# A two-layer diffusion block in split fp32: instruction order at the seams between stages, and weight buffers in pools of one and two slots

## The chip, the cores and the metric

The kernel runs on one core of a Trainium2 chip. The metric is the device time of one execution in microseconds; where several were measured, the median counts. The kernel before took 3605.2 us as the median of 3 runs (3592.66 to 3619.01).

## What is computed

A block of two layers over 256 latent tokens and 256 context tokens of width 2048, in fp32. Layer 0 mixes tokens with a bidirectional RWKV-7 scan, layer 1 with Hyena (long convolutions by Fourier transforms with filters from a small network). Around each mixer, and around the squared-ReLU MLP behind it, stand RMS norms and the modulation by `c` (adaLN).

```python
for i in range(DEPTH):                      # DEPTH = 2; context lives in layer 0 only
    mod = silu(c) @ ada_w[i] + ada_b[i]      # six rows of 2048
    h = rms_norm(x, norm_g[i, 0]) * (1 + mod[1]) + mod[0]
    y = rwkv_mixer(h, hc, ...) if i == 0 else hyena_stream(h, ...)
    x = x + mod[2] * rms_norm(y, norm_g[i, 1])
    h = rms_norm(x, norm_g[i, 2]) * (1 + mod[4]) + mod[3]
    x = x + mod[5] * rms_norm(square(relu(h @ mlp_up[i])) @ mlp_down[i], norm_g[i, 3])

# rwkv_mixer: token shift xx, lora branches, keys, scan over tokens, readout
k = (h + xx * mu[2]) @ w_k ; v = (h + xx * mu[3]) @ w_v ; r = (h + xx * mu[0]) @ w_r
S = S * w_t - (S @ kk_t) b_t^T + v_t k_t^T ; o_t = S @ r_t      # per head, both directions
y = ((group_norm(o) + bonus) * gate) @ w_o
```

## The kernel before, in words

The whole block is one program of the class `Kern`. A scheduler orders the instructions of each engine when the program is built: it takes them in the order in which the code was traced, moved by priorities (`tc.high_priority(n)`); on the chip each engine then runs its own list in order. Side work (adaLN products, filters, mixes) comes as Python generators that `tick` advances a little at a time between pieces of the main work; `self.rate` says how fast.

**Products.** Each fp32 matmul is three products of halves: an operand is cast by ACT to a high half (`wh`, `xh`, `yh`) and DVE subtracts it for the low half (`wl`, `xl`, `yl`) in `split_into`; `mm3` makes hi·hi, hi·lo and lo·hi into one PSUM tile. `load_split` takes a raw weight buffer (`w`, 128x2048), loads it on SP's queue, and splits it in tiles of 128x1024 (`wh`, `wl`). Raw buffers and split tiles come from lists of pools, `self.wraw` and `self.wsp`; `turn` rotates the list, so that the pools are taken in turn, and a pool of n slots gives its next slot out again when the tile n turns before has been used up. `open_weights(es, raw, sp)` adds one pool to each list. Before, the stages from w_o on use one pair of pools (raw 2 slots, split 3), and each MLP adds a pair of its own (`MLPW`, raw 1, split 3).

**Stages**, with their times in the profiled execution. 0 to 196 us: `start`, adaLN rows (`ada_first`), norms (`rstd`), the shifted tokens (`sx`, `shifted`), and for each of 16 chunks k the mixes (`xt`, `xh`, `xl`) for the decay, the iclr and the gate branch, whose products accumulate in six PSUM tiles; for `k < KEARLY` the mix for w_k is made in the same loop. To 431: the hidden layer of the branches, the w_k product (`rwkv_proj`, `gemm_ws`), beside it adaLN products by DVE (`acc`, `ada_run`) and more mixes. To 555: `rwkv_begin`, the first fills of r and v (w_r, w_v products, `fl`) and the second halves of the lora branches (`self.low`). To about 1403: the scan in eight groups of four heads (`rwkv_scan`), operands `VU`, `NT`, `KB`, `ard`; its list is pinned in traced order on PE, ACT, DVE and SP. The last group has the Hyena filters beside it (`filters`: three sine layers, then eight pairs of products with w4, split in `w4h`, `w4l`, and transforms stored as `ko`); then the last readout. To 1506: `rwkv_out`, y loaded (`yt`), split (`yh`, `yl`) and multiplied by w_o (`gemm_tok`). Then `resid` (sum of squares `ss`, root, reciprocal, two diagonal matrices `dg`, by which PE transposes and scales y, then the sum into x and the next norm), the first MLP (to 2294), `resid`, Hyena (to 2828), `resid`, the second MLP (to 3586), `resid`.

**Order around the change.** SP's queue carries most loads, the weights' and the scan's, in one list; what waits at its head holds back all behind it. ACT has the casts, the PSUM copies, `aw` (an adaLN chunk scaled for POOL to add) and the squares; DVE has the subtractions and the mixes.

Of the kernel before, what the change touches and what calls it, by code (L numbers as in the profile page):

```python
# [18 lines left out]
P = 128  # L19
# [50 lines left out]
class Kern:  # L70
# [105 lines left out]
    def gemm_ws(self, W, K, ms, x, ntok, evac, lead=False):  # L176

        nk = K // P
        if lead:
            ps = [[self.mm.tile([P, 512], F32, name="mm") for _ in range(2)] for _ in range(2)]  # L180
            for k0 in range(0, nk, 4):
                w = [self.load_split(W[k0 * P : (k0 + 4) * P, m0 * P : (m0 + 2) * P].rearrange("(k p) n -> p k n", p=P), 4, 256)
                     for m0 in ms[:2]]
                for k in range(4):
                    for j in range(2):
                        for i in range(2):
                            self.mm3(ps[j][i][:, :ntok], self.cut(w[j][k], slice(i * P, (i + 1) * P)), x(k0 + k),
                                     k0 + k == 0, k0 + k == nk - 1)
                self.tick(self.rate)
            for j in range(2):  # L190
                for i in range(2):
                    evac(ms[j] + i, ps[j][i][:, :ntok])
            ms = ms[2:]
        for m0 in ms:
            ps = [self.mm.tile([P, 512], F32, name="mm") for _ in range(2)]
            for k0 in range(0, nk, 8):
                src = W[k0 * P : (k0 + 8) * P, m0 * P : (m0 + 2) * P].rearrange("(k p) n -> p k n", p=P)
                w = self.load_split(src, 8, 256)
                for k in range(8):
                    for i in range(2):  # L200
# [3 lines left out]
                self.tick(self.rate)  # L204
            for i in range(2):
                evac(m0 + i, ps[i][:, :ntok])

    def gemm_tok(self, W, x, evac, lead=False, stages=None):

        for ns in ((0, 1), (2,), (3,)) if lead else ((0,), (1,), (2,), (3,)):  # L210
            ps = {(n, tt): self.mm.tile([P, 512], F32, name="mm") for n in ns for tt in range(2)}
            for k0 in range(0, KT, 4):
                if stages and len(ns) > 1:
                    stages(k0)
                for n in ns:
                    w = self.load_split(W[k0 * P : (k0 + 4) * P, n * 512 : (n + 1) * 512].rearrange("(k p) n -> p k n", p=P), 4, 512)
                    for k in range(k0, k0 + 4):
                        for tt in range(2):
                            self.mm3(ps[n, tt], self.cut(x(k), slice(tt * P, (tt + 1) * P)), w[k - k0], k == 0, k == KT - 1)
                    self.tick(self.rate)  # L220
            for n in ns:
                for tt in range(2):
                    evac(n, tt, ps[n, tt])
# [118 lines left out]
    def ada_scan(self, n, pool):  # L342
# [4 lines left out]
        nc.vector.memset(wide, 0.0)  # L347
        nc.vector.tensor_copy(wide[:, :, 0], self.sc2[:, 0, :])
        pick = pool.tile([P, 2], F32, name="pick", bufs=1)
        nc.vector.memset(pick, 0.0)  # L350
        for j in range(4):
            nc.vector.tensor_tensor(pick, pick, self.ident[:, 32 * j : 32 * j + 2], op=ALU.add)
# [42 lines left out]
    def rstd(self, x, pool, acc=None, make=None):  # L395
# [7 lines left out]
        for k in range(len(x)):  # L403
            if make:
                make(k)
            sq = pool.tile([P, L], F32, name="sq", bufs=3)
# [21 lines left out]
    def resid(self, x, y, ss, layer, gi, ch, pool, nxt=None):  # L428
# [12 lines left out]
        for n in range(1, 4):  # L441
            nc.vector.tensor_tensor(ss[:, 0, :], ss[:, 0, :], ss[:, n, :], op=ALU.add)
        nc.scalar.activation(ss[:, 1, :], ss[:, 0, :], AF.Sqrt, bias=self.eps[:, 0:1], scale=1.0 / D)
        nc.vector.reciprocal(ss[:, 1, :], ss[:, 1, :])
        dg = pool.tile([P, 2, P], F32, name="dg", bufs=1)
        for tt in range(2):
            nc.vector.tensor_scalar(dg[:, tt], self.ident, ss[:, 1, tt : tt + 1], None, op0=ALU.mult)
# [33 lines left out]
    def filters(self, es):  # L481
# [3 lines left out]
        p2 = self.pool(es, "f2", 2)  # L485
        fw = p1.tile([33, 64], F32, name="fw")
# [10 lines left out]
        for m, (lhs, n) in enumerate(((fw[:], 64), (w23[:], 64), (w3[:].rearrange("p a b -> p (a b)"), P))):  # L497
# [13 lines left out]
            if m == 2:  # L511
                self.tables()
            yield
# [9 lines left out]
        dft = []  # L523
        for i, nm in enumerate(("dftc", "dfts")):
            dft.append(self.dft_load(nm, p1, p2, "hf", 3))
        w4s = []

        def load(i):
            dc, o = divmod(i, 2)
            if dc < 4:  # L530
                w4 = p2.tile([P, 512], F32, name="w4")
                for b in range(2):
                    c0 = (b * 2 + o) * D + dc * 512
                    nc.sync.dma_start(w4[64 * b : 64 * b + 64, :], I["f_w4"][0, :, c0 : c0 + 512])
                w4s.append(w4)

        def skip(i):
            dc, o = divmod(i, 2)
            if dc < 4:
                self.sk = p2.tile([P, 512], F32, name="sk", bufs=1)[0:1, :]  # L540
                nc.sync.dma_start(self.sk, I["skip"][0, o : o + 1, dc * 512 : (dc + 1) * 512])

        def window(dc):
            if dc < 4:
                self.win = p2.tile([P, 2, 512], F32, name="win", bufs=1)
                nc.sync.dma_start(self.win, I["window"][:, dc * 512 : (dc + 1) * 512].rearrange("(a p) d -> p a d", p=P))

        window(0), load(0), skip(0)

        def first(dc, o, e, put):  # L550

            if not e:
                w4 = w4s.pop(0)
                self.w4 = split2(w4)
                load(2 * dc + o + 1)
            for tt in range(2):
# [4 lines left out]
                if o and e and tt:  # L561
                    window(dc + 1)
                if e == 0 and tt == 0:
# [6 lines left out]

        def split2(x):
            return self.split_into(p2.tile([P, 512], F32R, name="w4h")[:], x[:], p2.tile([P, 512], F32R, name="w4l")[:])
# [85 lines left out]
    def shifted(self, k):  # L658
# [3 lines left out]
        t = self.xt.tile([P, 512], F32, name="sx", bufs=2)  # L662
# [85 lines left out]
    def rwkv_proj(self, l2, ad1):  # L748
# [6 lines left out]
        self.bg, self.rate = [self.beside(mixed, self.NLOW + 24, ad, n)], (self.NLOW + 24 + n) / 15  # L755
# [17 lines left out]
        self.gemm_ws(I["w_k"][0], D, range(0, KT, 2), lambda k: xs[k], 512, evk)  # L773
# [179 lines left out]
    def rwkv_begin(self):  # L953
# [5 lines left out]
        for _ in self.beside(itertools.chain(self.fill_v(0), self.fill_r(1)), 48, self.low, n - n // 8 + .1):  # L959
            self.tick(self.BEG)  # L960
# [3 lines left out]
    def rwkv_scan(self, es, prep_pools, ngroups=KT // 2):  # L964
# [13 lines left out]
        self.bg, self.rate = [], 0.0  # L978
        for _ in self.scan_products(0, 0):
# [3 lines left out]
        for i in range(2):  # L983
            self.scan_values(0, i)
        self.pins = {}
        for g in range(ngroups):
# [88 lines left out]
    def scan_open(self, es, prep_pools):  # L1075

        self.loaded, self.unit, self.rx, self.due = [], 0, [], []
        self.ard, self.yf, self.kbp = [None] * 2, [None] * 2, [None] * 2
        self.scan_operands(self.pool(es, "so0"), 0)
        self.ge = self.pool(es, "sge", 2)  # L1080
# [316 lines left out]
    def scan_readout(self, g):  # L1397
# [53 lines left out]
    def rwkv_out(self, xp):  # L1451
        nc, tc = self.nc, self.tc
        with tc.tile_pool(reuse_waits="tile", name="oy", bufs=16) as oy, tc.tile_pool(reuse_waits="tile", name="op", bufs=1) as op:
            ys = []
            for k0, n in ((0, 4), (4, 4), (8, 4), (12, 2), (14, 2)):
                hi = [oy.tile([P, L], F32R, name="yh") for _ in range(n)]
                lo = [oy.tile([P, L], F32R, name="yl") for _ in range(n)]
                t = oy.tile([P, 4, L], F32, name="yt", bufs=2)
# [3 lines left out]
            ss = op.tile([P, 4, 2], F32, name="ss")  # L1462

# [7 lines left out]
            self.resid(x, o, ss, 0, 1, 2, op, (0, 2, 3))  # L1471
            return x
# [40 lines left out]
    PRT = 1  # L1513
# [4 lines left out]
    KEARLY = 16  # L1518
# [7 lines left out]
    SLACK = 0  # L1526
# [127 lines left out]
    def start(self, ap, xp):  # L1654
# [16 lines left out]
        self.pins, self.pinned = {}, ("pe",)  # L1671
# [5 lines left out]
        for q in range(4):  # L1677
# [4 lines left out]
            for k in range(4 * q, 4 * q + 4):  # L1682
# [5 lines left out]
                sx = self.shifted(k)  # L1688
                for n, m in enumerate((1, 4)):
# [8 lines left out]
        self.xs += [self.mix_split(2, k, True, self.xm) for k in range(self.KEARLY, KT)]  # L1698
# [27 lines left out]
    def run(self):  # L1726
        nc, tc = self.nc, self.tc
        with ExitStack() as es:
# [141 lines left out]
```

## Time and profile before

| what | us |
|---|---|
| median of 3 runs | 3605.2 |
| the profiled execution's own time | 3607.2 |
| its span (granted clock 0.968) | 3605.3 |
| TensorE (PE) busy | 3326.2 |
| VectorE (DVE) busy | 2457.0 |
| ScalarE (ACT) busy | 1739.7 |
| GpSimd (POOL) busy | 435.0 |

The profile is of one execution. Its page gives each engine's busy time; the table by stage gives the same for windows of the span; the waits name an engine's instruction, what it waited for, and the sum, the count and the longest wait in us; the timeline gives one row for an instruction or a run of equal ones, with its start, its length, and in brackets the idle time ahead of it and what ended it; the chain lists what ended last. PEld is TensorE's weight load, which runs beside the matmuls, L111 the line on which all split products are recorded, L53 that of the ACT, DVE and SP instructions.

### The profile page before, as it was taken

What the parts mean: (1) busy time and instruction counts of PE and PEld (TensorE: products, weight loads), DVE (VectorE), ACT (ScalarE), POOL (GpSimd) and SP (SyncE); (2) the same over time, 40 slices, a digit from 0 to 9 for tenths busy, and PEclk for the clock granted to TensorE, in tenths of its full rate; (3) what the DMA queues carried; (4) which work ended last, traced back from release to release, by engine and by line L of the source; (5) the groups of instructions that cost most, each with busy time, mean ns of one, the idle gap of its engine ahead of it and who ended that gap; (6) DMA issues with size and microseconds to landing.
All of it is one profiled execution on the core that took longest, in us unless ns stands there. A gap on an engine that the chain in (4) does not pass through costs nothing.

```text
span 3605.3 us, 74531 instructions
## 1 busy us (share of the span) xinstructions
PE 3326.2 (92%) x30598; PEld 2904.8 (81%) x30598; DVE 2457.0 (68%) x3867; ACT 1739.7 (48%) x3069; POOL 435.0 (12%) x496
## 2 busy tenths in 40 slices
PE   6799978989989788999999999999999899999999
PEld 3477777878888666898978889899887798989897
DVE  4788675767767655687777776587787675555554
ACT  4454454544544444443434435566664663434343
POOL 0011121111111000000000002034441540000000
PEclk8999998999999989999999999999999999999999
DMA  9678798988988635688888887566665775555553
GB/s 305 229 232 266 252 329 252 282 267 262 288 269 267 194 124 184 198 269 280 257 286 259 283 268 233 164 221 219 222 209 182 244 249 191 183 187 187 187 185 120
DMA packets 587807, 836.79 MB, mean 232 GB/s; under 512 B 39551, under 2 KB 373280, under 8 KB 587464
## 3 DMA queue, kind: packets, MB, share of 16 engines
q1 hardware_dynamic: 556360, 718.76, 62.1%
q0 software_dynamic: 31104, 113.26, 10.0%
q8 instruction: 239, 3.92, 0.5%
q14 instruction: 104, 0.85, 0.1%
HBM read 777.31 MB, written 54.59 MB: 231 GB/s over the span
## 4 chain that ended last, share of the span: by engine, by line
PE 49%; DMA 21%; DVE 14%; ACT 6%; issue 6%; POOL 2%; SPq 1%; ACTq 0%; DVEq 0%; POOLq 0%
PE mm L111 34%; DMA aw<-in_ada_w 10%; PE fl L111 5%; PE sg L111 5%; PE sc L111 4%; DVE wl L53 3%; DMA w<-in_mlp_down 2%; DVE acc L53 2%; DMA w<-in_mlp_up 2%; POOL acc L325 2%; ACT wh L53 2%; DVE tmp L53 1%; ACT aw L53 1%; DVE d L53 1%; DMA a<-a 1%
## 5 line engine op out<-in xcount | busy, mean ns | idle before, releaser
L53 DVE TENSOR_TENSOR wl<-w,wh 128x1024 fp32r<-128x1024 f32 (+1 forms) x716 | 918.6, 1288 | 548.7 <-ACT wh L53 546.8
L53 ACT CAST wh<-w 128x1024 fp32r<-128x1024 f32 (+1 forms) x716 | 738.1, 1043 | 744.4 <-PE mm L111 436.2
L111 PE MATMUL mm<-hxh,wh 128*128 128x258 f32 x2816 | 803.5, 287 | 13.2 <-DVE nt L53 11.9
L111 PE MATMUL mm<-hxh,wl 128*128 128x258 f32 x2816 | 801.5, 285 | 6.8 <-DVE wl L53 6.7
L111 PE MATMUL mm<-hxl,wh 128*128 128x258 f32 x2816 | 799.4, 284 | 0.0
L111 PEld LDWEIGHTS mm<-hxh,wh 128*128 128x128 f32 x2816 | 534.2, 190 | 17.0 <-DVE nt L53 13.8
L111 PEld LDWEIGHTS mm<-hxh,wl 128*128 128x128 f32 x2816 | 534.1, 190 | 10.7 <-DVE wl L53 9.3
L111 PEld LDWEIGHTS mm<-hxl,wh 128*128 128x128 f32 x2816 | 536.3, 190 | 1.8
L325 POOL TENSOR_TENSOR acc<-acc,aw 128x512 f32<-128x512 f32 x180 | 274.9, 1528 | 1360.2 <-ACT aw L53 1254.1
L111 PE MATMUL mm<-wh,uh 128*128 128x512 f32 x1024 | 405.4, 396 | 1.0 <-DVE nt L53 1.0
L111 PE MATMUL mm<-wl,uh 128*128 128x512 f32 x1024 | 400.5, 391 | 4.2 <-DVE wl L53 4.1
L111 PE MATMUL mm<-wh,ul 128*128 128x512 f32 x1024 | 402.3, 393 | 0.0
L53 DVE SCALAR_TENSOR_TENSOR acc<-aw,sc,acc 128x512 f32<-128x512 f32 x300 | 225.3, 751 | 89.6 <-DMA aw<-in_ada_w 87.0
L111 PEld LDWEIGHTS mm<-wl,uh 128*128 128x128 f32 x1024 | 192.3, 188 | 51.1 <-DVE wl L53 8.3
L111 PEld LDWEIGHTS mm<-wh,ul 128*128 128x128 f32 x1024 | 192.1, 188 | 45.6
L111 PEld LDWEIGHTS mm<-wh,uh 128*128 128x128 f32 x1024 | 192.3, 188 | 42.5 <-DVE nt L53 1.4
L111 PE MATMUL fl<-fh,fx 128*128 128x256 f32 x1024 | 213.1, 296 | 9.9 <-DMA fx<-xv 8.4
L53 ACT ACTIVATE aw<-aw,sc 128x512 f32<-128x512 f32 x180 | 125.8, 719 | 138.1 <-DMA aw<-in_ada_w 137.6
L111 PEld LDWEIGHTS fl<-fh,fx 128*128 128x128 f32 x1024 | 168.2, 193 | 27.9 <-issue 14.0
L111 PE MATMUL fl<-flo,fx 128*128 128x256 f32 x512 | 146.0, 285 | 0.4 <-issue 0.4
L111 PE MATMUL sg<-ard,KB 64*64 64x64 f32 (+1 forms) x3584 | 131.1, 247 | 13.5 <-ACT yf L53 4.8
L111 PE MATMUL mm<-xl,wh 128*128 128x512 f32 (+1 forms) x320 | 131.7, 412 | 12.1 <-DVE xl L53 12.0
(352 smaller groups left out, 5871.8 us busy)
## 6 DMA issues: line engine op xcount, KB each, us to landing
aw<-in_ada_w SPq DMA_DIRECT2D x288, 512.0 KB, 5.7
w<-in_mlp_down SPq DMA_DIRECT2D x128, 1024.0 KB, 5.1
w<-in_mlp_up SPq DMA_DIRECT2D x120, 1024.0 KB, 6.0
fx<-xv POOLq DMA_DIRECT2D x128, 512.0 KB, 6.2
aw<-in_ada_w SPq DMA_DIRECT2D x192, 256.0 KB, 3.0
w<-in_hy_in_w SPq DMA_DIRECT2D x44, 1024.0 KB, 6.2
fx<-xr POOLq DMA_DIRECT2D x64, 512.0 KB, 5.6
w<-in_w_k SPq DMA_DIRECT2D x16, 1024.0 KB, 5.7
```

The source lines that it names most:

```text
L53: return self.kern.pin(self.key, f(*a, **kw))
L111: return self.pin("pe", self.nc.tensor.matmul(out, lhsT=lhsT, rhs=rhs, **kw))
L325: nc.gpsimd.tensor_tensor(acc, acc, w[:, a], op=ALU.add)
```

## The change

The arithmetic and the number of instructions stay the same, but for one more small activation. What changes:

- *First stages.* `KEARLY` 16 to 12: the last four mixes for w_k come behind the loop, from the kept `sx` tiles (now 4). `self.mixed`, behind which the adaLN loads of the next stage are placed, is now the last of these. `rstd` has five `sq` buffers. The first block of w_k goes to PSUM tiles of the pool `sc` and advances no side work; side work runs at a rate of /13 in place of /15.
- *Begin and scan.* `LOWS` moves the lora branches ahead; the first two `scan_values` (the `VU` loads) are traced ahead of the first products, at priority 1000, as are the constants of the scan's adaLN; all remaining filter and adaLN work is taken ahead of the last readout, which uses `sc` tiles for both pairs.
- *Filters.* The loads of w4, window, skip and transforms are issued earlier, and w4 is split one step ahead.
- *Products.* In the last chunk of a product the output blocks are finished one after the other (`gemm_ws` with lead: by j; `gemm_tok`: by token half); `PRT` 1 to 400 for the last evacuations and for the chain up to `dg`.
- *Buffers.* The stages from w_o on have two pairs of pools: one of raw 1 and split 2 slots, opened ahead of `rwkv_out`, and one of raw 1 and split 1; `rwkv_out` opens its own second pair behind `yt`. The MLPs add (1, 3) as before. Since `turn` rotates the list, `open_weights` now takes its pool out by identity.

```diff
-                l.append(self.pool(es, n, b))
-                es.callback(l.pop)
+                p = self.pool(es, n, b)
+                l.append(p)
+                es.callback(lambda l=l, p=p: l.pop(next(i for i, q in enumerate(l) if q is p)))
...
+                order = [(j, k) for k in range(4) for j in range(2)]
+                for j, k in sorted(order) if k0 == nk - 4 else order:
...
-            ps = [self.mm.tile([P, 512], F32, name="mm") for _ in range(2)]
+            ps = first or [self.mm.tile([P, 512], F32, name="mm") for _ in range(2)]
...
+                    pairs = [(k, tt) for k in range(k0, k0 + 4) for tt in range(2)]
+                    for k, tt in sorted(pairs, key=lambda p: p[1]) if k0 == KT - 4 else pairs:
+                        self.mm3(ps[n, tt], self.cut(x(k), slice(tt * P, (tt + 1) * P)), w[k - k0], k == 0, k == KT - 1)
...
+            with self.tc.high_priority(self.PRT if 3 in ns else 0):
+                for n in ns:
+                    for tt in range(2):
+                        evac(n, tt, ps[n, tt])
...
+        with self.tc.high_priority(self.PRT):
+            for n in range(1, 4):
+                nc.vector.tensor_tensor(ss[:, 0, :], ss[:, 0, :], ss[:, n, :], op=ALU.add)
+            nc.scalar.activation(ss[:, 1, :], ss[:, 0, :], AF.Sqrt, bias=self.eps[:, 0:1], scale=1.0 / D)
+            nc.vector.reciprocal(ss[:, 1, :], ss[:, 1, :])
+            for tt in range(2):
+                nc.vector.tensor_scalar(dg[:, tt], self.ident, ss[:, 1, tt : tt + 1], None, op0=ALU.mult)
...
+        def weights(i):
+            halves.append(split2(w4s.pop(0)))
+            load(i)
...
+        window(0), load(0), load(1), skip(0)
...
-                w4 = w4s.pop(0)
-                self.w4 = split2(w4)
-                load(2 * dc + o + 1)
+                self.w4 = halves.pop(0)
...
+                if e and tt and w4s:
+                    weights(2 * dc + o + 3)
...
-        t = self.xt.tile([P, 512], F32, name="sx", bufs=2)
+        t = self.xt.tile([P, 512], F32, name="sx", bufs=4)
...
-        for _ in self.beside(itertools.chain(self.fill_v(0), self.fill_r(1)), 48, self.low, n - n // 8 + .1):
+        for _ in self.beside(itertools.chain(self.fill_v(0), self.fill_r(1)), 48, self.low, self.LOWS * (n - n // 8)):
...
+        with self.tc.high_priority(self.PRS):
+            for i in range(2):
+                self.scan_values(0, i)
         for _ in self.scan_products(0, 0):
             pass
         self.load_to(3 + self.AHEAD)
         self.feed_open(ngroups)
-        for i in range(2):
-            self.scan_values(0, i)
...
+        take(fill, 99), take(ada, 99)
         for _ in late:
             due, self.due = self.due, []
-            take(fill, 2)
             for f in due:
                 f()
-        take(fill, 99), take(ada, 99)
...
-            tile_ = lambda: (self.sc if last and pi else self.sg).tile([P, 512], F32, name="sc" if last and pi else "sg")
+            tile_ = lambda: (self.sc if last else self.sg).tile([P, 512], F32, name="sc" if last else "sg")
...
     def rwkv_out(self, xp):
...
+            es = ExitStack()
+            self.open_weights(es, 1, 1)
...
+                t = oy.tile([P, 4, L], F32, name="yt", bufs=2)
                 hi = [oy.tile([P, L], F32R, name="yh") for _ in range(n)]
                 lo = [oy.tile([P, L], F32R, name="yl") for _ in range(n)]
-                t = oy.tile([P, 4, L], F32, name="yt", bufs=2)
...
+            nc.scalar.activation(op.tile([P, 2], F32, name="st"), t[:, 1, :2], AF.Sqrt, scale=0.0, bias=self.eps[:, 0:1])
...
+            es.close()
...
-    PRT = 1
+    PRT = 400
...
-    KEARLY = 16
+    KEARLY = 12
...
+    LOWS = 1.25
+    PRS = 1000
...
-        self.xs += [self.mix_split(2, k, True, self.xm) for k in range(self.KEARLY, KT)]
+        self.xs += [self.mix_split(2, k, True, self.xm, sxs[k]) for k in range(self.KEARLY, KT)]
...
-                self.open_weights(e1)
-                self.np = self.pool(e1, "np", 1, "right")
-                self.hx = [self.np.tile([P, KT, L + 2], F32R, name=n, bufs=1) for n in ("hxh", "hxl")]
+
+                self.np = self.pool(e1, "np")
+                self.open_weights(e1, 1, 2)
+                self.hx = [self.pool(e1, n, 1, "right").tile([P, KT, L + 2], F32R, name=n, bufs=1) for n in ("hxh", "hxl")]
                 xp = self.pool(e1, "xp", side="right")
                 if self.upto >= 2:
                     x = self.rwkv_out(xp)
+                self.open_weights(e1, 1, 1)
```

How the order of instructions moves, at three places. DVE at the end of the lora stage: `acc` is the adaLN accumulation, `xt` a mix from `sx` and `hall`, `xl` the low half of its split; the last 256-wide `xl` is the gate branch's last split. Before:

```order
L53 SCALAR_TENSOR_TENSOR acc<-aw,sc_92,acc 128x512
L53 TENSOR_TENSOR xl<-xt,xh 128x512
L53 SCALAR_TENSOR_TENSOR xt<-sx,cols,hall 128x256
L53 SCALAR_TENSOR_TENSOR acc<-aw,sc_92,acc 128x512
L53 TENSOR_TENSOR xl<-xt,xh 128x512
L53 SCALAR_TENSOR_TENSOR xt<-sx,cols,hall 128x512
L53 TENSOR_TENSOR xl<-xt,xh 128x256
```

And now:

```order
L53 SCALAR_TENSOR_TENSOR xt<-sx,cols,hall 128x256
L53 TENSOR_TENSOR xl<-xt,xh 128x512
L53 SCALAR_TENSOR_TENSOR xt<-sx,cols,hall 128x512
L53 TENSOR_TENSOR xl<-xt,xh 128x512
L53 TENSOR_TENSOR xl<-xt,xh 128x256
L53 SCALAR_TENSOR_TENSOR xt<-sx,cols,hall 128x512
```

No `acc` stands between the last splits any more, and the last mixes for w_k (the last row is one of them) follow the gate's split.

SP at the start of the scan: `VU` are the first groups' values, `r` the store of a fill, `fr` the fill's weights, `gate` a store of the lora branch. What leaves is marked -, what comes +:

```order
-L53 DMA fr<-in_w_v 128x2x256
-L53 DMA gate<-l2t 128x256
-L53 DMA fr<-in_w_v 128x2x256
+L53 DMA VU<-v 64x128 x12
 L53 DMA r<-fe 128x2x256
-L53 DMA fr<-in_w_v 128x2x256
-L53 DMA VU<-v 64x128 x12
+L53 DMA fr<-in_w_v 128x2x256 x3
 L53 DMA aw<-in_ada_w 128x4x256 x2
```

The twelve `VU` loads stand ahead of the store of `r` and of three `fr` loads.

ACT at the start of the last group: `wh<-w` are casts of w_o's weights, `yf`, `rhs`, `KR`, `VU` copies of the scan. Before:

```order
L53 COPY rows<-mm 128x256
L53 CAST wh<-w 128x1024 x3
L53 COPY yf<-sg 32x16x32 x2
L53 COPY rhs<-sc 128x256
L53 COPY KR<-sg 128x4x64 x2
L53 ACTIVATE VU<-sc 64x2x2x64 x2
L53 ACT_TABLE_LOAD
```

And now:

```order
L53 COPY rows<-mm 128x256
L53 COPY yf<-sg 32x16x32 x2
L53 COPY rhs<-sc 128x256
L53 COPY KR<-sg 128x4x64 x2
L53 ACTIVATE VU<-sc 64x2x2x64 x2
L53 ACT_TABLE_LOAD
L53 ACTIVATE fz_16942<-fa 64x256
L53 CAST dftch<-hf 128x512
L53 COPY Z<-sc 128x256
```

The three casts are gone from here; the casts of the transform (`dftch`) and of w4 stand earlier.

More of the change, by code (lines that the diff above doesn't have):

```diff
@@ L174, in split_into, with gemm_ws @@
         return hi, lo
-    def gemm_ws(self, W, K, ms, x, ntok, evac, lead=False):
+    def gemm_ws(self, W, K, ms, x, ntok, evac, lead=False, first=None):
         nk = K // P
@@ L203, in gemm_ws @@
                                  k0 + k == 0, k0 + k == nk - 1)
-                self.tick(self.rate)
+                if not first:
+                    self.tick(self.rate)
             for i in range(2):
                 evac(m0 + i, ps[i][:, :ntok])
+            first = None
     def gemm_tok(self, W, x, evac, lead=False, stages=None):
@@ L346, in ada_scan @@
         wide = pool.tile([P, KT, 32], F32, name="wide", bufs=1)
[L347 to L348 removed]
         pick = pool.tile([P, 2], F32, name="pick", bufs=1)
[L350 to L352 removed]
+        with self.tc.high_priority(self.PRS):
+            nc.vector.memset(wide, 0.0)
+            nc.vector.tensor_copy(wide[:, :, 0], self.sc2[:, 0, :])
+            nc.vector.memset(pick, 0.0)
+            for j in range(4):
+                nc.vector.tensor_tensor(pick, pick, self.ident[:, 32 * j : 32 * j + 2], op=ALU.add)
         todo = [(layer, ch, i, half, k4) for layer, ch, i in itertools.islice(self.ada_todo, n) for half in range(2) for k4 in range(4)]
@@ L405, in rstd @@
                 make(k)
-            sq = pool.tile([P, L], F32, name="sq", bufs=3)
+            sq = pool.tile([P, L], F32, name="sq", bufs=5)
             nc.scalar.activation(sq[:, :n], x[k], AF.Square)
@@ L485, in filters, with load, skip, window @@
         p2 = self.pool(es, "f2", 2)
+        w4s = []
+        def load(i):
+            dc, o = divmod(i, 2)
+            if dc < 4:
+                w4 = p2.tile([P, 512], F32, name="w4")
+                for b in range(2):
+                    c0 = (b * 2 + o) * D + dc * 512
+                    nc.sync.dma_start(w4[64 * b : 64 * b + 64, :], I["f_w4"][0, :, c0 : c0 + 512])
+                w4s.append(w4)
+        def skip(i):
+            dc, o = divmod(i, 2)
+            if dc < 4:
+                self.sk = p2.tile([P, 512], F32, name="sk", bufs=1)[0:1, :]
+                nc.sync.dma_start(self.sk, I["skip"][0, o : o + 1, dc * 512 : (dc + 1) * 512])
+        def window(dc):
+            if dc < 4:
+                self.win = p2.tile([P, 2, 512], F32, name="win", bufs=1)
+                nc.sync.dma_start(self.win, I["window"][:, dc * 512 : (dc + 1) * 512].rearrange("(a p) d -> p a d", p=P))
+        def weights(i):
+            halves.append(split2(w4s.pop(0)))
+            load(i)
+        def split2(x):
+            return self.split_into(p2.tile([P, 512], F32R, name="w4h")[:], x[:], p2.tile([P, 512], F32R, name="w4l")[:])
+        halves, dft = [], []
+        window(0), load(0), load(1), skip(0)
         fw = p1.tile([33, 64], F32, name="fw")
@@ L512, in filters @@
                 self.tables()
+            else:
+                nm = ("dftc", "dfts")[m]
+                dft.append(self.dft_load(nm, p1, p2, "hf", 3))
+            if m == 1:
+                weights(2)
             yield
@@ L771, in evk @@
                                  start=m == 0 and x is sh, stop=m == KT - 1 and x is sl)
-        self.gemm_ws(I["w_k"][0], D, range(0, KT, 2), lambda k: xs[k], 512, evk)
+        self.gemm_ws(I["w_k"][0], D, range(0, KT, 2), lambda k: xs[k], 512, evk, first=[self.sc.tile([P, 512], F32, name="sc") for _ in range(2)])
         ri = ev.tile([P, 512], F32, name="kt")[:NH]
@@ L978, in rwkv_scan @@
         self.bg, self.rate = [], 0.0
+        with self.tc.high_priority(self.PRS):
+            for i in range(2):
+                self.scan_values(0, i)
         for _ in self.scan_products(0, 0):
@@ L1688, in start @@
                 sx = self.shifted(k)
+                sxs[k] = sx
                 for n, m in enumerate((1, 4)):
```

50 lines of the change are left out of this document (5 added, 45 removed).

## The prediction

> **What bounds the kernel now.** I read the page first, then the busy time of each engine by stage, then the waits and the timeline at every stretch in which TensorE stands still.
>
> ```profile
> PE 3326.2 (92%) x30598; PEld 2904.8 (81%) x30598; DVE 2457.0 (68%) x3867; ACT 1739.7 (48%) x3069; POOL 435.0 (12%) x496
> ```
>
> TensorE is the bound: 3326 of 3605 us. The change removes no matmul, so it can only touch the 279 us in which PE is idle, or add to them. Where these lie, the table by stage says (columns: window, its length, busy time of each engine with its instructions, granted clock, DMA share, GB/s):
>
> ```profile
> 160.00:196.00 36.00, 20.67 (x89) 13.70 (x87) 35.35 (x61) 17.97 (x29) 0.00 (x0) 0.91 0.50 152
> 196.00:431.00 235.00, 225.56 (x960) 180.65 (x960) 184.39 (x287) 105.89 (x170) 35.84 (x49) 0.96 0.79 260
> 555.00:575.00 20.00, 8.08 (x115) 6.97 (x116) 6.83 (x17) 6.74 (x15) 0.54 (x1) 0.57 0.69 209
> 1240.00:1262.00 22.00, 12.19 (x326) 9.34 (x319) 9.94 (x18) 10.47 (x18) 0.00 (x0) 0.67 0.59 179
> 1262.00:1403.00 141.00, 120.65 (x1348) 90.76 (x1348) 76.23 (x143) 64.16 (x139) 0.00 (x0) 0.91 0.38 122
> 1403.00:1434.00 31.00, 19.88 (x74) 15.06 (x74) 15.40 (x30) 13.78 (x25) 0.00 (x0) 0.89 0.90 293
> 1506.00:1560.00 54.00, 43.41 (x307) 41.53 (x306) 43.97 (x77) 26.59 (x55) 0.00 (x0) 0.92 0.77 239
> 1560.00:2294.00 734.00, 720.57 (x4529) 648.86 (x4527) 533.75 (x718) 312.62 (x461) 23.94 (x17) 0.99 0.80 262
> 2340.00:2828.00 488.00, 458.67 (x3173) 423.65 (x3172) 378.71 (x476) 295.10 (x472) 191.78 (x167) 0.99 0.67 218
> 2828.00:2840.00 12.00, 2.01 (x9) 1.53 (x9) 6.39 (x8) 6.68 (x13) 5.87 (x6) 0.63 0.86 273
> ```
>
> The seven short rows (all but 196 to 431, 1560 to 2294 and 2340 to 2828) are the seams that the diff names: length less PE's busy time gives 15.3 + 11.9 + 9.8 + 20.4 + 11.1 + 10.6 + 10.0 = 89 us. That is the ceiling on what closing them can bring. The long rows are dense: the first MLP leaves PE idle for 13.4 us of 734, the hyena for 29.3 of 488.
>
> **The change part by part.**
>
> *End of the lora stage.* DVE is busy for 35.35 of 36 us and PE waits for its splits:
>
> ```profile
> PE mm L111 <- DVE xl L53: 10.8, 6, 3.5
> ```
> ```profile
> L53 DVE SCALAR_TENSOR_TENSOR acc<-aw,sc,acc x11: 742/743/752, 164.5 to 192.2; 128x512 f32<-128x512 f32 x11
> ```
> ```profile
> 188.28 0.74 DVE L53 SCALAR_TENSOR_TENSOR acc<-aw,sc,acc 128x512 f32<-128x512 f32 x1
> 188.94 0.68 DVE L53 TENSOR_TENSOR xl<-xt,xh 128x512 fp32r<-128x512 f32 x1
> ```
>
> Start to start an `acc` takes 0.66 us. Ten of the eleven stand ahead of the last split; they now stand behind it: 10 x 0.66 = 6.6 us. The last four mixes for w_k leave the loop too, each an `xt` and an `xl` (0.66 + 0.6 us, start to start): 5.0 us. DVE has 12 us less to do before PE's last lora product; then ACT, which waited for DVE here, is late next, so I take 8. The same 12 us of DVE work run under w_k, where DVE has 235 - 184 = 51 us free and PE is idle for 9.4: 2 us given back, between 0 and 12. Net -6 us, between -15 (all idle time of the window) and 0.
>
> *Scan start.* SP's queue holds the operands back:
>
> ```profile
> 556.00 0.37 SPq L53 DMA_DIRECT2D r<-fe  x1
> 556.93 9.27 SPq L53 DMA_DIRECT2D VU<-v  x12
> ```
> ```profile
> PE sc L111 <- DMA VU<-v: 7.5, 1, 7.5
> ```
>
> The twelve VU loads, which the first products of the scan read, stand behind the store of `r`. Now they stand ahead of it. The store and three `fr` loads are pushed behind 9.27 us of issue, but nothing in the first pieces of the scan reads them. What is late next is the ada load and the `NT` mask. -7 us of the 11.9, between -11 (all but a hand-off) and 0 (if the VU buffers only come free then).
>
> *Last group and filters.* ACT and DVE are stuck behind casts of w_o's weights that have not landed:
>
> ```profile
> 1239.95 10.46 DMA w<-in_w_o
> ```
> ```profile
> PE sg L111 <- ACT yf L53: 4.8, 1, 4.8
> ...
> PE sc L111 <- issue: 4.6, 1, 4.6
> ```
>
> Behind the casts stand the `yf` copies, for which PE waits; now no cast of w_o stands there, and the 9.4 us of these two rows become 1.5: -8, between -9.4 and 0 (`dftch` and `w4h` casts now stand earlier on ACT, ahead of a `Z` copy, and wait for loads themselves). In the filters the split of w4 is made one step ahead:
>
> ```profile
> PE sg L111 <- ACT w4h L53: 8.4, 6, 2.2
> ```
>
> -8, between -8.4 and 0: the cast keeps its length, it only leaves the chain. Together -16.
>
> *Readout and w_o.* The y loads are issued earlier, and the last readout takes two more PSUM tiles:
>
> ```profile
> PE mm L111 <- ACT yh L53: 7.4, 1, 7.4
> ```
> In the new order the first two `yt` loads and the first w_o load stand ahead of the last two stores of y, but still behind ten stores of the filters. -6 us, between -11.1 and 0.
>
> *Seams of resid.* The sums, the root and `dg` come under priority, and the last chunk finishes one token half first:
>
> ```profile
> PE sg L453 <- DVE dg L53: 5.3, 1, 5.3
> ```
> ```profile
> PE sg L453 <- DVE dg L53: 10.0, 1, 10.0
> ```
> ```profile
> 2831.55 1.33 ACT L53 ACTIVATE aw<-aw,sc 128x512 f32<-128x512 f32 x2 [2.93 <-DMA aw<-in_ada_w]
> ```
>
> The first row is the seam at 1506, the second that at 2828, where ACT sits 2.9 us for an ada load and then runs two `aw` before the last square; those still stand there, so only part of the 10 goes. -2.5 and -4; the two ends of the MLPs, whose chain is the same, 1.5 each: -9.5, between -18 and 0.
>
> *Clock.* After the idle 3.05 us in front of it, the first product of w_k is slow:
>
> ```profile
> 196.50 0.79 PE L111 MATMUL mm<-xh,wh 128*128 128x512 f32 x1 [3.05 <-ACT xt L53]
> ```
>
> ```profile
> L111 PE MATMUL mm<-wh,uh 128*128 128x512 f32 x1024 | 405.4, 396 | 1.0 <-DVE nt L53 1.0
> ```
>
> 0.79 us here, 0.40 for the common 512-wide product. With the granted clock at 0.57 to 0.67 in three of the short rows I add -3 for time that counts as busy, between -8 and 0. [...]
>
> Sum of the seams: -6 - 7 - 16 - 6 - 9.5 - 3 = -47.5 us.
>
> *What it adds: buffers with one slot.* Weights are split by ACT (`wh`) and then DVE (`wl`):
>
> ```profile
> 1487.32 1.05 ACT L53 CAST wh<-w 128x1024 fp32r<-128x1024 f32 x1 [0.29 <-PE mm L111]
> ```
> ```profile
> 1488.41 1.23 DVE L53 TENSOR_TENSOR wl<-w,wh 128x1024 fp32r<-128x1024 f32 x1 [1.18 <-ACT wh L53]
> ```
>
> From the cast's start to the end of the subtraction are 2.32 us; with the hand-offs 2.5. Before, w_o and the hyena turn through one pool of three slots. Now two pools are taken in turn, of two slots and of one, so every second tile goes to the one slot: its cast can't begin until the tile before last is used up, and it must be done when the tile between is. Cover is the time of one tile, not two. In the MLPs three pools (1, 2 and 3 slots) are taken in turn: cover of two tiles for every third, where it was five for all. What queues behind such a waiting cast on ACT are the next tile's cast, the evacuations of the same stage and the ada products, for which DVE and POOL wait. The number of subtractions by stage gives a tile's time (columns: window, length, DVE busy with count):
>
> ```profile
> 1434.00:1506.00 72.00, 32.52 (x28) 0.98 0.56 185
> 1560.00:2294.00 734.00, 305.01 (x245) 0.99 0.80 262
> 2340.00:2828.00 488.00, 176.18 (x122) 0.99 0.67 218
> ```
>
> w_o: 72/28 = 2.6 us, just the 2.5. Hyena: 4.0 on average, slack 1.5; w_o's and hyena's shortest tiles have none. MLPs: 2 x 3.0, slack 3.5. No row of before shows a cast on such a slot, so the price is bounded. Below: 0, if ACT is always free when the slot is. Above, by what ACT waits for:
>
> ```profile
> ACT aw L53 <- DMA aw<-in_ada_w: 103.7, 56, 6.4
> ```
> ```profile
> ACT wh L53 <- DMA w<-in_mlp_down: 127.1, 25, 11.2
> ...
> ACT wh L53 <- DMA w<-in_mlp_up: 104.7, 22, 12.2
> ```
> ```profile
> L53 ACT ACTIVATE aw<-aw,sc 128x512 f32<-128x512 f32 x180 | 125.8, 719 | 138.1 <-DMA aw<-in_ada_w 137.6
> ```
>
> Hyena (first row): a cast behind one ada wait (103.7/56 = 1.85) and its `aw` (0.72) is 2.57 late, 1.07 beyond the slack; some 52 one-slot tiles (half of 122, less the next MLP's first): 56 us. The waits fill only 21% of the window, but the out-projection has no slack: about a third of it, 20. First MLP: a wait for `w` lasts 231.8/47 = 4.9, 1.4 beyond the slack, on a third of 47: 22 at most; its raw buffers now turn 1+1+1 and refill earlier than 2+1, so 5. w_o: 14 tiles x 0.6 (one more small operation of ACT) = 8 at most, 2 taken. Second MLP, where waits are short: 1, at most 5. Sum +28, between 0 and 91.
>
> *Sum.* The profiled execution took 3607.2 us (span 3605.3), 2.0 over the median: 3607.2 - 47.5 + 28 = 3587.7, so 3586 as a median.
>
> **The rivals.** *Slots are hidden* (chance 0.30): ACT is busy for 295 of the hyena's 488 us and takes each cast at once; then the seams alone count: 3605.2 - 47.5 = 3558. For it speaks that the hyena's PE waits little for splits now; against, that it has three slots now. *One slot bites* (0.13), the slower one: in the hyena each one-slot cast lands behind an ada wait, and the full 91 us are paid: 3605.2 - 47.5 + 91 = 3649. The change loses from the point where slots cost over 47.5, with 8 elsewhere 0.76 us on each of the hyena's 52. For it: ACT waits 56 times there; against: only a fifth of the time. [...] *Seams move instead of closing* (0.17): the next releaser stands right behind the removed one (ada loads at 2828, the ten stores ahead of `yt`, ACT at the lora end). Half the gain, 24, against 28: 3609.
>
> **How the numbers follow.** My forecast, slots biting at the tight tiles, has 0.40: 3586. Its own spread is some 20 us. Within 1% (3569 to 3641) is what a measurement of this kernel can tell from no change. Faster by over 1%: 0.26 from hidden slots, 0.09 from the forecast's lower end, 0.01 from moved seams: 0.36. Slower: 0.10 from biting slots, 0.02 from the forecast and 0.04 from moved seams with them: 0.16. The rest, 0.48, is within 1%. Range 3545 to 3640: below 3558 by part of the clock and lora bounds, above up to nearly the biting slots.
>
> **What would show it.** Right: no PE wait for VU near 563, no w_o cast in the last group, w4h gone from the list of waits, `dg` waits under 6 us, PE's idle time in the short windows down from 89 to some 45; and in the hyena PE's waits for `wl`, in sum, up by about 20 us. Wrong, if those waits stay under 8 us (hidden slots), exceed 45 us (biting), or if the short windows still hold over 65 us (moved seams).

## The result, and the profile after

The change made the kernel slower: 3622.7 us against 3601.3 us for the kernel before, medians of 20 runs each, a ratio of 1.0058 (95% interval 1.0045 to 1.0072). That is +21 us where -19.5 was forecast, and the other sign. The profiled execution took 3614.25 us, 8 under its median; that of before was 6 over its own. A profile is one execution, so single profiles are read by stage here, and totals come from the repeated runs.

The page after, first line of its table of busy time:

```profile
PE 3333.7 (92%) x30598; PEld 2905.5 (80%) x30598; DVE 2434.7 (67%) x3867; ACT 1738.6 (48%) x3070; POOL 436.2 (12%) x496
```

PE is busy 7.5 us longer for the same matmuls, and idle for as long as before (279 us). So the idle time did not go, it moved: in the windows of the seven seams, taken where they now lie, PE is idle for 57 us in place of 89, and behind them it is idle for longer. Marks in the two profiles, by the start or end of PE's products, say where (us; the last column is what the stretch up to the mark lost or gained):

| reached | before | after | stage |
|---|---|---|---|
| end of the lora products | 193.5 | 185.8 | -7.6 |
| end of w_k | 430.7 | 424.6 | +1.5 |
| first `sc<-VU,NT` of the scan | 562.8 | 551.4 | -5.4 |
| end of the last group's inversion (`sg<-d,d`) | 1244.6 | 1224.9 | -8.2 |
| end of the filters | 1402.6 | 1360.4 | -22.6 |
| first product of w_o | 1410.4 | 1370.9 | +2.8 |
| end of w_o | 1506.3 | 1472.0 | +5.1 |
| first product of the first MLP | 1514.9 | 1480.4 | -0.3 |
| end of its products | 2294.2 | 2290.2 | +30.6 |
| end of the hyena's products | 2828.7 | 2832.1 | +7.4 |
| end of the second MLP's | 3586.5 | 3594.3 | +4.5 |

Up to the first MLP the change is 34.6 us ahead. The first MLP alone takes 30.6 of that back. The waits of PE in it, before:

```profile
PE mm L111 <- DVE nt L53: 11.2, 7, 3.7
PE mm L111 <- DVE wl L53: 5.2, 8, 1.5
```

and after:

```profile
PE mm L112 <- DVE wl L53: 26.2, 21, 4.7
PE mm L112 <- ACT wh L53: 4.4, 5, 1.5
PE mm L112 <- DVE nt L53: 2.6, 2, 1.8
```

PE now waits for split weights. I matched each product of this stage to the address of the tile that it reads: of the 26 gaps of PE over 0.3 us in front of such a product, 20 are at the buffer of the pool with one slot, and 29.1 of their 34.7 us. The largest but one, as DVE sees it (timeline after; `acc` is the adaLN accumulation):

```profile
1643.04 1.53 DVE L53 SCALAR_TENSOR_TENSOR acc<-aw,sc,acc 128x512 f32<-128x512 f32 x2
1649.00 0.75 DVE L53 SCALAR_TENSOR_TENSOR acc<-aw,sc,acc 128x512 f32<-128x512 f32 x1 [4.43 <-DMA aw<-in_ada_w]
1649.67 0.68 DVE L53 COPY o<-mm 128x512 f32<-128x512 f32 x1
1650.27 0.74 DVE L53 SCALAR_TENSOR_TENSOR acc<-aw,sc,acc 128x512 f32<-128x512 f32 x1
1650.93 1.22 DVE L53 TENSOR_TENSOR wl<-w,wh 128x1024 fp32r<-128x1024 f32 x1
```

as ACT sees it:

```profile
1645.43 1.05 ACT L53 CAST wh<-w 128x1024 fp32r<-128x1024 f32 x1 [5.45 <-PE mm L112]
```

and PE:

```profile
1646.97 0.71 PE L112 MATMUL mm<-wh,uh 128*128 128x512 f32 x2
1652.20 0.67 PE L112 MATMUL mm<-wl,uh 128*128 128x512 f32 x1 [4.52 <-DVE wl L53]
```

ACT waited for the one slot and cast at once, at 1645.43. DVE could have subtracted at 1646.5, but it stood at an `acc` whose ada load landed at 1648.9; behind that `acc`, a copy and another `acc`, at 1650.93, came the turn of `wl`. With more slots the same waiting of DVE should do no harm, since the tile is split long before its use; the first experiment shows it.

The seams, after, each line of another wait list (scan start; last group, twice; w_o; the resid at 1472 and that at 2832):

```profile
PE mm L112 <- DMA aw<-in_ada_w: 6.7, 1, 6.7
```
```profile
PE sg L112 <- DMA z<-in_zfeat: 1.8, 1, 1.8
...
PE sg L112 <- ACT yf L53: 1.5, 1, 1.5
```
```profile
PE mm L112 <- ACT wh L53: 7.5, 1, 7.5
```
```profile
PE sg L460 <- DVE dg L53: 2.6, 1, 2.6
```
```profile
PE sg L460 <- DVE dg L53: 6.5, 1, 6.5
```

The wait for VU is gone, and one for the ada load (6.7 us) stands in its place; the last group's 9.4 us became 3.3, the six waits for `w4h` are no longer in the list (one of 4.2 us for the filters' `zsh` is); in front of w_o `yh` (7.4) gave way to `wh` (7.5); the two `dg` waits shrank by 2.7 and 3.5.

### The profile page after: what moved, and what is told of

Same layout as the page of the kernel before. It is cut to its first block, busy times and chain, and to the rows that moved or that the text cites. A ratio compares the mean times of both kernels' runs of the same rounds, so it can differ in the third digit from the quotient of the medians.

```text
span 3612.5 us, 74494 instructions
## 1 busy us (share of the span) xinstructions
PE 3333.7 (92%) x30598; PEld 2905.5 (80%) x30598; DVE 2434.7 (67%) x3867; ACT 1738.6 (48%) x3070; POOL 436.2 (12%) x496
## 4 chain that ended last, share of the span: by engine, by line
PE 39%; DMA 26%; DVE 19%; ACT 8%; issue 7%; POOL 1%; SPq 1%; DVEq 0%; ACTq 0%; POOLq 0%
PE mm L112 25%; DMA aw<-in_ada_w 10%; DVE wl L53 6%; DMA w<-in_mlp_up 5%; PE sg L112 4%; PE fl L112 4%; PE sc L112 3%; DMA w<-in_mlp_down 3%; ACT wh L53 3%; DVE acc L53 2%; DVE tmp L53 1%; DVE d L53 1%; ACT aw L53 1%; POOL acc L330 1%; DVE xt L53 1%
## 5 line engine op out<-in xcount | busy, mean ns | idle before, releaser
L53 DVE TENSOR_TENSOR wl<-w,wh 128x1024 fp32r<-128x1024 f32 (+1 forms) x716 | 896.2, 1268 | 511.2 <-ACT wh L53 509.5
L53 ACT CAST wh<-w 128x1024 fp32r<-128x1024 f32 (+1 forms) x716 | 728.3, 1043 | 717.1 <-PE mm L112 344.9
L112 PE MATMUL mm<-wh,uh 128*128 128x512 f32 x1024 | 390.5, 397 | 1.3 <-DVE nt L53 0.8
L112 PE MATMUL mm<-xl,wh 128*128 128x512 f32 (+1 forms) x288 | 116.6, 405 | 11.4 <-DVE xl L53 11.4
```

Of the source, the lines that this page charges most:

```text
L53: return self.kern.pin(self.key, f(*a, **kw))
L112: return self.pin("pe", self.nc.tensor.matmul(out, lhsT=lhsT, rhs=rhs, **kw))
```

## The experiments

Each ratio is to the kernel before on the same chip, with its 95% interval. All of them left the computation as it is, except e9 and e10.

**Is it the one-slot buffer?** First kernel, e1: every pool stands in the list once for each slot.

```diff
-                l.append(p)
-                es.callback(lambda l=l, p=p: l.pop(next(i for i, q in enumerate(l) if q is p)))
+                l.extend([p] * b)
+                es.callback(lambda l=l, p=p: l.__setitem__(slice(None), [q for q in l if q is not p]))
```

> The change as it is, but each pool stands in the list once for each of its slots, so that the slots are used in turn and not the pools: cover is two tiles in w_o and hyena and five in the MLPs, as before the change. Theory of the slots (the one-slot pools eat what the seams gain, above all in the first MLP): the first MLP's 810 us fall back to about 780, PE's waits for wl there from 26 to about 5 us, and the time is about 3565 (between 3555 and 3575). Rival (the earlier start of the first MLP collides with its own loads, whatever the slots): it stays near 3620, with the first MLP at 800 us or more.

Measured: 0.9883 (0.986 to 0.9907), 3556.4 us against 3601.6: 42 to 45 us under before and some 63 under the change, with the same memory, the same tiles and the same work. The first MLP takes 757.6 us, less than before's 779.2. PE's waits there (all that the list has of `mm`):

```profile
PE mm L112 <- DVE nt L53: 3.8, 1, 3.8
...
PE mm L112 <- ACT hxh L53: 0.2, 1, 0.2
```

No wait for `wl` is left, and the theory of the slots holds against the collision. DVE still waits at `acc` as long as in the change (there 88.7 us in 49 waits):

```profile
DVE acc L53 <- DMA aw<-in_ada_w: 87.0, 47, 4.0
```

So the late ada loads are there in both kernels; only with the one slot do they reach PE. That the kernel beats the expected 3565 and before's own first MLP needed another cause (e5).

**The pools alone (e2).** The kernel before with nothing but the change's pools:

```diff
-                self.open_weights(e1)
-                self.np = self.pool(e1, "np", 1, "right")
+                self.np = self.pool(e1, "np")
+                self.open_weights(e1, 1, 2)
...
+                self.open_weights(e1, 1, 1)
```

> The kernel before with nothing but the change's pools for weights. Theory of the slots: slower than before by 45 to 60 us, about 3650, with the first MLP at about 810 us. Rival (collision of the earlier start): within 10 us of before, about 3605.

Measured: 1.0075 (1.005 to 1.01), 3625.8 us, first MLP 796.0. A loss without any seam, so no collision is needed; but 24 to 27 us, half of what was expected. The last group and the filters took 149.2 us here in place of 158.1. The casts of w_o's weights have left the last group, as the prediction said; but e5 below, which leaves them there, takes 149.9 us for the same stretch, so no run shows that this is what the 9 us come from.

**The seams with the old pools (e3).** The change with before's lines of `run` and no pair of w_o's own.

> The change with the weight pools of before (one pair, raw 2 and split 3 slots) and no pair of w_o's own. Theory of the slots: the seams' gain without their price, 3565 to 3575, a little worse than the even turn because w_o's weights come late again in the last group. Rival (collision): 3610 to 3620.

Measured: 0.9936 (0.9913 to 0.9959), 3577.7 us, just above the range expected. The seams alone are worth 23 us (15 to 31), not 47.5.

**A fresh pair behind w_o (e4).**

```diff
-                self.open_weights(e1, 1, 2)
+                ew = ExitStack()
+                self.open_weights(ew, 1, 2)
...
-                self.open_weights(e1, 1, 1)
+                ew.close()
+                self.open_weights(e1)
```

> The change up to the end of w_o; there both pairs of pools are closed and one pair of raw 2 and split 3 slots is opened for the rest. Theory of the slots: w_o keeps its 101 us, the first MLP falls to about 780 and the out-projection of the hyena back by 6, so 3570 to 3580. Rival (collision): 3610 to 3620. If the first loads of the MLP come late because they wait for the closed pools, the seam behind w_o grows by up to 6 us.

Measured: 0.9918 (0.9898 to 0.9938), 3568.9 us, within the range expected; w_o keeps its 99.3 us, the first MLP takes 771.8, and the seam behind w_o did not grow (2.6 + 3.1 us). The first MLP is 14 us above e1's, though both have six split slots in turn: what differs in this stage is the raw buffers, 2 and 1 in turn by pool here, three in turn there. The next kernel tests that.

**The raw buffers of the kernel before (e5).** Before, with the even turn alone.

> The kernel before with nothing but the even turn. Its split slots are used evenly already (3 and 3), its raw buffers in the MLPs are not (pools of 2 and 1 in turn: one buffer for every second load). Theory (uneven raw buffers cost the kernel before too): the first MLP falls from 779 to about 758 us and the second from 744 to about 740, so the time is about 3577. Rival (the 22 us that the even turn gained over the first MLP of before came with the seams, not with the raw buffers): within 6 us of before, the first MLP at 775 or more.

Measured: 0.9944 (0.9924 to 0.9964), some 20 us under before; first MLP 755.8, second 739.1. ACT's waits for the MLP's weights there, over 230 us before, are 9.9 us here. The kernel before lost 20 us to a raw pool of one slot that had every second load. The change had ended this without aiming at it: its three raw pools of one slot each, in turn, are three slots evenly.

**How many slots, or the shortest cover (e6)?** The even turn with `MLPW = (1, 1)`.

> The even turn of e1 with two split slots fewer in each MLP (MLPW 1, 1): four slots, cover of three tiles for all, where the change has six slots and cover of two tiles for every third. Theory (the shortest cover decides, not the number of slots): first MLP at 760 to 775 us, time 3557 to 3575, well under the change. Rival (the number of slots decides): first MLP at 810 or more, time over 3620.

Measured: 0.9889 (0.9865 to 0.9913), 3552.9 us, first MLP 763.4. Four slots in even turn are as good as six in the whole time, and both far better than the change's six in uneven turn. The shortest cover decides, not the number.

**Why the first MLP and not the second?** The change (e9) and e1 (e10) with `ADA[2]` 16 to 0, so that the adaLN blocks beside the first MLP are left out. Each ran once.

> The change without the sixteen adaLN blocks that run beside the first MLP (they are left out: 128 loads of 512 KB, DVE's acc, and their results stay zero or move). Read against e10. Theory (a one-slot cast is late where the queues are held by loads that land late): the first MLP loses most of its price; it is within 12 us of that of e10, as the second MLP is (751 against 739). Rival (the one slot costs by itself, with ACT and DVE free): 30 us or more over e10.

> The even turn of e1 with the same sixteen blocks left out of the first MLP. Both theories: its first MLP at 740 to 755 us, near the 739 of the second, which has four blocks.

Measured, first MLP of the change without the blocks, then of e1 without them (table by stage):

```profile
1484.00:2222.00 738.00, 736.47 (x4687) 668.51 (x4686) 406.20 (x512) 332.76 (x491) 0.13 (x2) 1.00 0.55 181
```
```profile
1472.00:2205.00 733.00, 733.00 (x4688) 668.68 (x4687) 410.69 (x513) 334.90 (x492) 0.13 (x2) 1.00 0.56 182
```

738.7 against 733.5 from mark to mark. With the blocks it is 809.8 against 757.6. The price of the one slot falls from 52 to 5 us: the slot alone costs little, and what it costs is the lateness of the queues that refill it. With the blocks go DVE's `acc`, but also their 128 loads (the DMA share is 0.55 here, 0.76 with them), and no run parts the two. For DVE's queue speaks that ACT still waits 138 us for `w` in e9 (167 in the change), and PE only 1.4 us for `wl`. In the change's own profile, 14.4 of the 29.6 us that PE spends in waits over 0.3 us for split tiles come behind an `acc` that stood for its load; in the rest DVE was running an `acc` or another subtraction, or the cast itself was late.

**Which seams paid?** From e1, parts undone one by one. The seams of resid (e8; again as e15, beside its base e14, which is e1 once more; e16 with the order by token half kept):

```diff
-    PRT = 400
+    PRT = 0
...
-                    for k, tt in sorted(pairs, key=lambda p: p[1]) if k0 == KT - 4 else pairs:
+                    for k, tt in pairs:
```

> The even turn of e1 (1.17% under before) with the seams of resid undone: no priority for the last evacuations and the chain to dg, and the last chunk of gemm_tok in the old order. The prediction's term says that they are worth 9.5 us: it would be that much slower than e1, about 0.9% under before. What the profile of the change shows (the four seams together changed by about 4 us, and e1's own by less): within 4 us of e1, about 1.1% under before.

> The even turn of e1 once more, as the base for the three kernels beside it: 1.1 to 1.3% under before. Both theories.

> The even turn without the seams of resid (no priority, old order of the last chunk), as e8, now beside its base. Theory (the resid part is a loss of some 15 us, as e8 against e1 reads across two chips' runs): 0.3 to 0.5% under e14. Rival (e8 was another chip's luck; its profiled execution is 6 us under that of e1, and no stage differs by more than 4): within 0.2% of e14.

> The even turn without the priority, but with the last chunk in the order by token half. If the resid part is a loss, this tells which half of it: with the order (it holds each split tile of the last chunk until the second token half, so slots come free later) it stays with e14; with the priority it goes with e15. Rival: within 0.2% of both.

Measured: e8 0.9842 (0.9812 to 0.9872), which looked like a gain from undoing; side by side e14 0.9868 (0.9846 to 0.989), e15 0.9852 (0.9827 to 0.9877), e16 0.9879 (0.9858 to 0.99). All intervals overlap: the resid part moves nothing that these runs can tell, and the larger distance of e8 from e1 did not come again.

The last readout beside the filters again, with the old PSUM tiles (e11):

> The even turn of e1 with the last readout traced as before, two pieces of the filters to each of its pieces, and with the old PSUM tiles for it. The profile of the change shows the readout now standing behind the filters, with 8 us of idle PE in front of w_o (a gate load of 5.7 us in the chain) where before had 7.4. Theory (the readout was only moved, not shortened: nothing gained there): within 5 us of e1, on either side. Rival (the prediction's 6 us are real and hidden in the shorter filter stage): 5 to 10 us slower than e1.

Measured: 0.9879 (0.9852 to 0.9907), as e1. From the inversion mark to w_o's first product are 151.3 us here and 150.1 in e1: the readout was moved, not shortened.

The start of before (`KEARLY` 16, rate /15, two `sx`, three `sq`, no `first`; e12):

> The even turn of e1 with the start as before (KEARLY 16, the old rate, sx and sq buffers, no PSUM tiles of its own for the first block of w_k). The prediction's term and the profile of the change agree on about 6 us: 4 to 9 us slower than e1, about 1.0% under before. If the DVE work that moves under w_k is paid back in full: same as e1.

Measured: 0.9902 (0.9873 to 0.9931) against e1's 0.9883: 7 us by the medians' ratio, as expected, but within scatter; the profile has the end of the lora products at 195.8 us in place of 184.4.

The begin and the scan's start of before (no early VU loads, no priority, `LOWS` undone; e13):

> The even turn of e1 with the begin and the scan's start as before (no early VU loads, no priority, LOWS undone). The prediction's term says 7 us, the profile of the change 5: 4 to 8 us slower than e1, about 1.0% under before. If the scan's first group catches up later: same as e1.

Measured: 0.9862 (0.9837 to 0.9887), not slower than e1. Its scan starts 7 us later (556.3 against 549.3), but reaches the last group's inversion at 1230.1, where e1 has 1229.7.

What stays when resid part and begin are both undone (e17):

> The even turn with the resid part and the begin of the scan undone: what is left of the change are the start, the filters, the readout's order and the buffers. If e13 (0.2% under e1) and e8 are real, the fastest of the four, about 1.7% under before. If they are scatter between runs, within 0.3% of e14.

Measured: 0.9873 (0.9849 to 0.9898), as e14. The start, the filters with the last group, and the even turn reach the whole gain, as far as runs with intervals of some 9 us to either side can tell. Against e15, from which it differs by the begin alone, e17 is 8 to 10 us slower, within that scatter too; and its scan does not catch up: it starts at 561.9 and reaches the inversion at 1240.0, where e15 has 550.7 and 1227.7. So whether the begin is worth anything stays open.

## Why the prediction was wrong

**The balance.** Forecast: seams -47.5, slots +28. Measured in pieces: seams -23 (e3), raw buffers in even turn -20 (e5), split slots in uneven turn about +63 (the change, 1.0058, against e1, 0.9883). Together +20, and +21 was measured; the first two alone are -43, and e1, which has just these two, stands at -42. The rival with the biting slot came true in sign and in kind, a one-slot tile that is late behind an ada load; its place, the hyena, and its engine, ACT, were wrong. That 3622.7 lies inside the range stated is no merit of the forecast: the range reached almost to that rival.

**The step that failed most: the price of one slot.** The prediction took 5 us in the first MLP, "22 at most", 20 in the hyena, 2 in w_o and 1, "at most 5", in the second MLP. Against e1 by the profiles, the change loses 52 us in the first MLP, 12 in the second, 3 in the hyena and 8 in w_o (elsewhere the two profiles differ by some 13 us the other way). Two things were wrong in it. In the first MLP the lateness was taken from ACT's waits for `w` alone, and DVE's queue was left out. There the kernel before shows, between 1560 and 2294 us:

```profile
DVE acc L53 <- DMA aw<-in_ada_w: 62.8, 36, 5.2
```

36 waits of up to 5.2 us against a slack of 3.5 were the row to read; the largest gaps of the change lie behind such waits, and in e9, without them, the price is gone. And the upper bound spread each kind of wait over a third of the tiles, as if a late tile left the next one alone: a late split also frees its raw buffer late. In the second MLP, where ACT waited 9 us for `w_down` and 9 for `w_up` before, it now waits

```profile
ACT wh L53 <- DMA w<-in_mlp_down: 77.0, 21, 6.5
ACT wh L53 <- DMA w<-in_mlp_up: 76.7, 27, 5.9
```

so a loaded buffer that used to be there in time no longer is; e1, with the same three raw buffers, has no such wait in its list. The hyena was over-priced: PE's waits for split weights rose there, but 406.0 us stand against 404.9 before and 405.5 in e1 up to its out-projection, and the out-projection, where the prediction saw no slack, takes some 129 us against 123 and 127. Its ada products go to ACT and POOL, and other work of PE lies between its weight tiles; that this is the reason is not tested.

**Raw buffers.** The prediction saw that they "refill earlier" and lowered a price by it. It was a gain of its own, 20 us, visible in the kernel before as 127.1 and 104.7 us of ACT's waiting for `w`. A one-slot pool was there to be read before the change: before's MLPs had one, among the raw buffers.

**The seams, term by term** (forecast, then the two profiles). A mark of one profile can be off by some 10 us: e2 and e5 run before's code up to the last group of the scan, and reach the first `sc<-VU,NT` at 564.3 and 554.2, where before has 562.8.

- *Lora end:* -6; -7.6 and 1.5 given back under w_k. Right, to the split of gain and return.
- *Scan start:* -7; -5.4 at the first product, then the ada load is late next, as the prediction named it. In the whole time it is not shown: e13, without this part, is no slower than e1, and e17 is slower than e15 by no more than the scatter.
- *Last group and filters:* -16; -22.6 against before's profile, and -14.4 against that of e5, whose code is the same up to here. Right, within what one profile can tell.
- *Readout and w_o:* -6; +2.8. Wrong. The `yt` loads came out of the way, but two gate loads of the readout stand behind them on SP, and DVE waits for one of them ahead of the first `wl`; the chain after:

```profile
1364.42 5.71 DMA sqo<-gate
...
1370.97 1.23 DVE wl L53
```

- *Resid:* -9.5; -2.7 at 1472 and -3.5 at 2832 in front of `dg`, then +2.4 and +0.5 back before the first product of the next stage, nothing at 2294; nothing in e15. Wrong in size: the wait for `dg` was shared with what comes next.
- *Clock:* -3, the author's estimate from the clocks of three short rows (0.57 to 0.67); no run shows this term alone. For the same matmuls PE is busy 12 us less up to the first MLP (1294.5 against 1306.5), at a granted clock of 0.95 against 0.94. The sign was right up to there; in the first MLP PE is busy 12 us more (772.8 against 760.9), at 0.98 against 0.99, and 8 more behind it.

The 8 us between the scan's start and the last group's inversion are not counted: this stretch, whose work is the same in all these kernels, takes 659.7 to 674.0 us from the first ada product to that mark.

What was said to show it: VU, w_o's casts and `w4h` did leave the waits; one `dg` wait stayed over 6 us (6.5), and the idle time at the seams fell to 57 us and not to 45; PE's waits for `wl` rose by 21 us, but in the first MLP, and not by 20 in the hyena.

What stays open: why uneven turn cost 47 us without the seams (e2 corrected by the raw buffers' 20) and 63 with them. The first MLP is 796.0 us in the one and 809.8 in the other; the intervals of the two differences nearly meet, and no run tells which part of the order does this.

A version that beats both kernels is e1, 0.9883, and 0.9868 when it was measured again as e14; e6 is as good with two slots fewer in each MLP.

## What to carry to other kernels

When buffers are split over several pools that are used in turn, the smallest pool sets the cover: put each pool in the list once for each slot, and a layout that lost 21 us gains 42 to 45. Price a shorter cover with the longest waits of every engine that refills the buffer, not of the first one only, and look for them in the stage with the fullest queues. And a gain at a seam counts only as far as the next stage does not wait there anyway.

## What had not been expected of the hardware

The granted clock fell to a half without an idle stretch as long as the 3.05 us ahead of the first, slow product of w_k in the kernel before. PE was idle for 1.10 us up to 1787.41 and again from 1788.50, for 0.78 us; the clock fell inside the second gap, at about 1788.9 (table by stage of the profile after):

```profile
1784.00:1786.00 2.00, 2.00 (x19) 2.00 (x18) 1.19 (x2) 1.64 (x2) 0.00 (x0) 1.00 0.82 247
1786.00:1788.00 2.00, 0.90 (x8) 0.69 (x7) 1.66 (x3) 2.00 (x5) 0.00 (x0) 1.00 0.79 227
1788.00:1789.00 1.00, 0.50 (x6) 0.41 (x4) 1.00 (x2) 0.37 (x1) 0.00 (x0) 0.95 0.29 109
1789.00:1792.00 3.00, 2.72 (x6) 2.15 (x7) 3.00 (x5) 1.02 (x2) 0.00 (x0) 0.50 0.20 23
1792.00:1793.00 1.00, 1.00 (x9) 0.99 (x8) 1.00 (x3) 0.15 (x1) 0.00 (x0) 0.84 0.74 258
```

The clock is 0.50 from there to 1792.3, for 3.4 us, and full again behind it. In the clock records of this trace the 38 whole stretches at half clock last 3.4 us (24 of them), 6.8 (9), 10.2 (4) or 27.3 us (1). What made the clock fall is not shown; ahead of it stood the two gaps, with eight products between them. Here the gaps were followed by a loss beyond their own length: in these 3.4 us the 512-wide products start 0.43 us apart (from 1789.87 to 1791.58), at full clock 0.23 us apart (from 2001.03 to 2005.17). The first MLP, by stage, after and in e1:

```profile
1480.00:2290.00 810.00, 773.03 (x4820) 696.61 (x4819) 575.62 (x786) 337.55 (x508) 24.59 (x17) 0.98 0.76 251
```
```profile
1483.00:2240.00 757.00, 751.39 (x4819) 686.85 (x4820) 576.33 (x783) 345.11 (x510) 23.12 (x17) 0.99 0.82 269
```

Of the 53 us between them 31 are idle time of PE (37.0 against 5.6); 22 are the same matmuls, longer, at a granted clock of 0.98 against 0.99. The clock explains about half of the 22: the stage spends 32 us at half clock after and 9 in e1, worth some 11 us, an estimate from the 0.43 and 0.23 us above; the rest stays open.
